# A dense layer's up products as 2x2 blocks with seven products for eight, on one core of Trainium2

## The chip, the core and the metric

The kernel runs on one core of a Trainium2 chip. A core has five engines with a row of instructions each: TensorE (PE: matmuls into PSUM; its weight loads are a row of their own, PEld), VectorE (DVE), ScalarE (ACT), GpSimd (POOL) and SyncE (SP), which issues the DMA transfers between the chip's memory and SBUF. Each engine takes its instructions in the order in which the program lists them and waits on semaphores for the others. The metric is the time of one execution on the device in microseconds, as the median of several executions.

## The reference, cut to what matters

Two layers, each a token mixer and a gated MLP with a convolution, on 1024 tokens of width 1024 with a hidden width of 22 x 128 = 2816, in float32. The change is in the second half of a layer and in the place of the modulations:

```python
for l in range(DEPTH):                                   # DEPTH = 2
    mod = (c_act @ w_mod[l] + b_mod[l])[:, None, :]
    sh1, sc1, g1, sh2, sc2, g2 = jnp.split(mod, 6, axis=-1)
...
    y = jnp.concatenate([oa, ob, oc, od], axis=-1) @ w_out[l]
    x = x + g1 * rms_norm(y, norm_g[l, 1])

    h = rms_norm(x, norm_g[l, 2]) * (1 + sc2) + sh2
    u = dwconv3(h @ w_up[l], ffn_conv[l])                # 1024 -> 2 x 2816, three taps along the tokens
    ug, uv = jnp.split(u, 2, axis=-1)
    y = (jax.nn.gelu(ug, approximate=True) * uv) @ w_down[l]
    x = x + g2 * rms_norm(y, norm_g[l, 3])
```

## The kernel before, in words

Features lie on the 128 partitions, tokens along the free dimension: a 128x1024 tile holds 128 features of all tokens, and "half 0" and "half 1" are the first and the last 512 tokens. Every float32 operand is held as two parts that TensorE can multiply, a high part and a low part. `split` (L108 to L111) makes them: ScalarE copies the high part (L110), and GpSimd or VectorE subtracts it for the low part (L111). A product is then three matmuls, high x high, high x low and low x high (`product`, L477, L478 and L481, and `mm3`, L468 to L470). The low and high parts of the normed input are the tiles `hh` and `hl`; the trace calls the tiles that share their room `hx` and `hp`.

The output projection of the mixer ends with the tiles `pw`. Then follow, for each half, a norm and a residual add (`residual`, L460 and L461), a second norm with modulation (`modulated`, L441 to L447) and the splits; a norm's sums over features are 8 or 7 matmuls with a tile of ones (L158), its scale a chain of small VectorE operations (`rstd`, L176 to L189). The modulated second half comes while TensorE does the first up products on half 0.

`ffn` goes over the 22 hidden tiles t in pairs. For a tile, a 1024x128 piece of the gate's weights and one of the value's are loaded (512 KB each) and split; 96 matmuls give both, 24 for each half of each; ScalarE copies PSUM to `u` (L1128); VectorE convolves both (`conv3`, L875 and L877), ScalarE applies the gelu (L1146), VectorE multiplies (L1147), and the result is split into `ah` and `al`. One pair later the down products of a pair run (`down_all`): eight output tiles of 128 features, 96 matmuls for each hidden pair, and VectorE adds each PSUM tile to the sums `y` (L1190). The last two pairs run by halves (`down`, L1168): half 0 of both, then the end of the layer for half 0, then half 1 of both, whose weights are still in SBUF, then its end. In layer 0 a half's end is a norm, the residual (written to memory, `xd`) and the modulated input of layer 1.

The modulations (`mod`, six pieces of 1024 per layer) are sums over eight rows of weights. `mod_sum` loads sixteen tiles of 256 KB (`mr`, two buffers, L357), eight for each of two sums, and VectorE adds them up (L360, L362); `mod_fold` transposes and reduces the two sums over the partitions (L402 to L416). In layer 0 six of them run in the background of the MLP: the last of layer 0 and five of layer 1.

The row of each engine is fixed when the program is built, by a scheduler that knows the program's order and the tiles' buffers; at run time it is not reordered. Pools give out their buffers in the order of the program, so an instruction can wait for a tile that is used by an unrelated earlier step.

## Time and profile before

| | |
|---|---|
| median of 3 executions | 3238.64 us (3237.59 to 3239.95) |
| the profiled execution's own time | 3236.76 us |
| its span, first to last instruction | 3234.9 us |
| granted TensorE clock, mean over the span | 0.974 |
| TensorE busy | 2985.9 us (92%) |
| VectorE, ScalarE, GpSimd busy | 63%, 33%, 30% |
| dense layer of layer 0, last `pw` to the last down product | about 869 to 1642 us |
| dense layer of layer 1 | about 2448 to 3216 us |

The profile shows one execution. Times of its rows count from the span's start. A busy share is an average over stages with different limits: TensorE's 92% holds stretches of 100% and stretches where it waits, and what a change in one stage is worth is read from that stage. Two instructions that follow each other on VectorE overlap by some 0.1 us, so a row with "x2" can be shorter than twice one.

### The profile page before, as it was taken

Reading aid. Unit: us, or ns where it says so; the run is one execution under the profiler, and the core shown is the slowest. Engines: PE = TensorE matmul, PEld = TensorE weight load, DVE = VectorE, ACT = ScalarE, POOL = GpSimd, SP = SyncE. Lnnn points to the kernel's source line nnn. Section 1 sums busy time; section 2 is a strip of 40 time slices with the busy share of each in tenths; the row PEclk is TensorE's granted clock in tenths of the full one; section 3 lists DMA queues with packets and bytes.
Section 4 is the critical chain, followed back from the end, with each engine's and each line's share of the span. In section 5 each row is a group of like instructions: output and inputs, shape, how many; then the busy total and the mean of one; then the engine's idle time right before and its main releaser. Section 6 shows DMA issues by size and latency. Waiting matters only on the chain. (4 is left out here: it accounts for less than half of the span.)

```text
span 3234.9 us, 35358 instructions
## 1 busy us (share of the span) xinstructions
PE 2985.9 (92%) x13706; PEld 2365.9 (73%) x13706; DVE 2029.7 (63%) x2849; ACT 1063.9 (33%) x1554; POOL 956.7 (30%) x712
## 2 busy tenths in 40 slices
PE   7888988988999999999988998898899999999997
PEld 3677767776677777788856886777676888888886
DVE  6687567698656666653587727568956434434347
ACT  4232443554332222212243324336534222222222
POOL 1221133324342322223232213142334422233222
PEclk9998999999999999999999998999999999999998
DMA  5235111103312433211131121110132111111113
GB/s 202 78 101 177 54 37 34 56 20 108 128 58 93 134 113 114 95 40 52 46 124 58 55 82 42 38 52 19 37 109 91 65 39 40 43 62 52 40 40 104
DMA packets 103091, 237.15 MB, mean 73 GB/s; under 512 B 11227, under 2 KB 29915, under 8 KB 102924
## 3 DMA queue, kind: packets, MB, share of 16 engines
q1 hardware_dynamic: 102924, 234.90, 22.4%
q8 instruction: 107, 1.75, 0.2%
q14 instruction: 60, 0.49, 0.1%
HBM read 205.59 MB, written 32.67 MB: 74 GB/s over the span
## 5 line engine op out<-in xcount | busy, mean ns | idle before, releaser
L111 POOL TENSOR_TENSOR wl<-raw,wh 128x1024 fp32r<-128x1024 f32 (+2 forms) x96 | 234.5, 2451 | 663.7 <-ACT wh L110 472.4
L477 PE MATMUL pj<-hp,uh 128*128 128x512 f32 x880 | 352.6, 401 | 1.6 <-ACT hp L442 1.6
L478 PE MATMUL pj<-hp,uh 128*128 128x512 f32 x880 | 347.1, 394 | 2.9 <-POOL hp L445 2.8
L477 PE MATMUL pj<-hh,wh 128*128 128x512 f32 x800 | 327.9, 410 | 14.2 <-DVE ql L526 8.5
L478 PE MATMUL pj<-hl,wh 128*128 128x512 f32 x800 | 323.2, 404 | 3.7 <-POOL hl L445 3.2
L481 PE MATMUL pj<-hp,ul 128*128 128x512 f32 x880 | 290.2, 394 | 0.0
L111 POOL TENSOR_TENSOR ul<-raw,uh 128x1024 fp32r<-128x1024 f32 x96 | 238.5, 2486 | 162.5 <-PE pj L481 84.7
L875 DVE TENSOR_SCALAR ta<-u,par 128x1024 f32<-128x1024 f32 (+1 forms) x46 | 55.9, 1216 | 356.1 <-ACT u L1128 324.0
L477 PE MATMUL pj<-hx,uh 128*128 128x512 f32 x528 | 212.5, 403 | 12.6 <-ACT u L1128 10.0
L110 ACT ACTIVATE wh<-raw 128x1024 fp32r<-128x1024 f32 (+2 forms) x104 | 107.2, 1047 | 345.1 <-PE po L469 242.8
L481 PE MATMUL pj<-hx,ul 128*128 128x512 f32 x528 | 209.8, 397 | 0.0
L478 PE MATMUL pj<-hx,uh 128*128 128x512 f32 x528 | 207.7, 393 | 0.0
L481 PE MATMUL pj<-hh,wl 128*128 128x512 f32 x800 | 206.5, 398 | 0.0
L477 PEld LDWEIGHTS pj<-hp,uh 128*128 128x128 f32 x880 | 165.6, 188 | 45.6 <-ACT hp L442 2.2
L478 PEld LDWEIGHTS pj<-hp,uh 128*128 128x128 f32 x880 | 165.5, 188 | 44.9 <-POOL hp L445 5.5
L481 PEld LDWEIGHTS pj<-hp,ul 128*128 128x128 f32 x880 | 165.2, 188 | 39.3 <-issue 1.0
L477 PEld LDWEIGHTS pj<-hh,wh 128*128 128x128 f32 x800 | 154.4, 193 | 54.0 <-issue 17.0
L110 ACT ACTIVATE uh<-raw 128x1024 fp32r<-128x1024 f32 x100 | 105.5, 1059 | 262.9 <-DMA raw<-in_w_up_dram 141.2
L1190 DVE TENSOR_TENSOR y<-y,po 128x1024 f32<-128x1024 f32 x96 | 117.0, 1219 | 110.6 <-PE po L470 110.6
L478 PEld LDWEIGHTS pj<-hl,wh 128*128 128x128 f32 x800 | 154.1, 193 | 41.8 <-POOL hl L445 5.4
L481 PEld LDWEIGHTS pj<-hh,wl 128*128 128x128 f32 x800 | 151.6, 190 | 34.6 <-issue 0.2
L1128 ACT ACTIVATE u<-pj 128x512 f32<-128x512 f32 x176 | 103.7, 593 | 209.1 <-PE pj L481 209.1
(375 smaller groups left out, 7120.2 us busy)
## 6 DMA issues: line engine op xcount, KB each, us to landing
raw<-in_w_up_dram SPq DMA_DIRECT2D x88, 512.0 KB, 3.5
mr<-in_w_mod_dram SPq DMA_DIRECT2D x144, 256.0 KB, 3.4
raw<-in_w_in_dram SPq DMA_DIRECT2D x52, 512.0 KB, 3.5
raw<-in_w_down_dram SPq DMA_DIRECT2D x44, 512.0 KB, 3.5
room<-in_w_mod_dram SPq DMA_DIRECT2D x48, 256.0 KB, 3.6
xd<-y SPq DMA_DIRECT2D x48, 256.0 KB, 2.4
raw<-in_w_out_dram SPq DMA_DIRECT2D x16, 512.0 KB, 3.9
x<-xd SPq DMA_DIRECT2D x14, 512.0 KB, 4.4
```

The lines of the kernel that those rows point to most:

```text
L110: self.nc.scalar.activation(hi, src, AF.Copy)
L111: (eng or self.nc.gpsimd).tensor_sub(lo, src, hi.bitcast(F32))
L477: nc.tensor.matmul(ps, wh[:, ks], self.hh[k][:, hs], start=k == 0, stop=False, skip_group_check=True)
L478: nc.tensor.matmul(ps, wh[:, ks], self.hl[k][:, hs], start=False, stop=False, skip_group_check=True)
L481: nc.tensor.matmul(ps, wl[:, ks], self.hh[k][:, hs], start=False, stop=k == KT - 1, skip_group_check=True)
L875: nc.vector.tensor_scalar(o, t[:, 0:n], cw(0), None, op0=ALU.mult)
L1128: nc.scalar.activation(u[:, 1 + 512 * half:513 + 512 * half], ps, AF.Copy)
L1190: self.mark = nc.vector.tensor_add(d, d, p)
```

## The change

The up products are regrouped. Let the 1024 input features be two halves (four tiles each) and the 1024 tokens two halves: the input is 2x2 blocks b11, b12, b21, b22, and the weights of a gate tile and a value tile are 2x2 blocks a11, a12, a21, a22. The product of two 2x2 block matrices is formed from seven block products, of sums of blocks, for eight. `dense_input` makes the normed second half into the sums t1 to t4 of input blocks (32 VectorE operations on 128x512, twelve GpSimd splits); `dense_up` goes over the 22 tiles: `sums` loads the gate's and the value's weights and makes the sums of weight blocks on VectorE (L1238 to L1243) with three or four splits; `begin` and `rest` issue seven quarters of twelve matmuls; five adds on VectorE combine them (L1268, L1275 to L1279). For the first five tiles `begin`, two of the quarters, is issued ahead. The gated tile is stored unsplit to memory (`actd`, L1289).

The down products form a second phase, `dense_down`, after all tiles: steps of two or four hidden tiles load weights and gated tiles, split them, multiply and add to `y`. In layer 0 the last eight hidden tiles are done by halves, four steps of two for half 0, then the end of the layer for half 0, then the same weights loaded once more for half 1. All background modulations move into this phase (six in layer 0, one in layer 1). A modulation's first sum stays on VectorE (L365, L367); its second is now scaled on ScalarE (L361) and added on GpSimd (L363); each of the two has one `mr` buffer of its own. The pool `fw` for weights has three buffers for four.

```diff
@@ mod_sum
-                    w = self.mr.tile([128, 512], F32, name="mr", tag="mr")
+                    w = self.mr.tile([128, 512], F32, name="mr", tag=f"mr{u}")
...
-                if k == 0:
+                if u and not room:
+                    nc.scalar.activation(w if k else acc, w, AF.Copy, scale=s)
+                    if k:
+                        nc.gpsimd.tensor_add(acc, acc, w)
+                elif k == 0:
@@ dense_input
+        n1, n2 = HALVES
+        self.t2, self.t3, self.t4w = [], [], []
+        for i in range(4):
+            j = 4 + i
+            a, b, t12 = y[i], y[j], temp("x")
+            t1, t2, t3, t4 = t12[:, n1], t12[:, n2], temp("sq"), temp("t")
+            normal(i)
+            normal(j)
+            shifted(j)
+            nc.vector.scalar_tensor_tensor(t1, a[:, n2], self.shift(l, 3, i), a[:, n1], op0=ALU.add, op1=ALU.subtract)
+            nc.vector.tensor_sub(t2, b[:, n2], t1)
+            nc.vector.tensor_sub(t4, b[:, n1], t2)
+            nc.vector.tensor_sub(t3, t2, a[:, n1])
+            self.split(self.hh[i][:, n2], self.hl[i][:, n2], t1, nc.vector)
+            self.split(self.hh[j][:, n2], self.hl[j][:, n2], b[:, n2])
+            for to, k, t, eng in ((self.t2, i, t2, None), (self.t4w, None, t4, nc.vector), (self.t3, j, t3, None)):
+                room = self.te.tile([128, 1024], F32R, name="t4", tag=f"t4{i}") if k is None else self.new_y(k, F32R)
+                self.split(room[:, n1], room[:, n2], t, eng)
+                to.append((room[:, n1], room[:, n2]))
@@ dense_up
+            def sums(t, whole):
...
+                nc.vector.tensor_add(s1, a21, a22)
+                nc.vector.tensor_sub(s2, s1, a11)
+                self.split(*w4, a22)
+
+                nc.vector.tensor_sub(a21, a11, a21)
+                nc.vector.tensor_sub(a22, a12, s2)
+                self.split(*w2, sums)
+                self.split(*w3, raw)
...
+                def tail(u):
+                    yb, z, w, u2 = (state[k] for k in ("y", "z", "w", "u2"))
+                    self.quarter(yb, w3, 0, t3, False)
+                    nc.vector.tensor_add(uv[:, c1], yb, u[:, c2])
+                    self.quarter(z, w3, 512, b22, False)
+                    nc.vector.tensor_add(u[:, c2], z, u2)
+                    nc.vector.tensor_add(uv[:, c2], uv[:, c2], uv[:, c1])
+                    nc.vector.tensor_add(uv[:, c1], uv[:, c1], w)
...
+            begun = [begin(early[t] if t < len(early) else self.up_weight(l, t)) for t in range(ahead)]
+            for t in range(FT):
+                w1, w2, w3, w4 = sums(t, t >= ahead)
+                if t < ahead:
+                    u, uv = begun[t], u_tile()
+                    head, tail = rest(u, w2, w3, w4, uv)
+                    head(u, t == 0)
+                else:
+                    uv = u_tile()
+                    head, tail = rest(None, w2, w3, w4, uv)
+                    u = begin(w1, head)
+                tail(u)
+                gated(t, (u, uv))
@@ dense_down
+            steps = [(2, "fwfw"), (4, "p" * 8), (4, "qqqqfwff")] + \
+                ([(2, "pppp")] * 4 if last else [(4, "p" * 8)])
+            mods = {0: (0, 5), 1: (1, 1), 2: (1, 0), 3: (1, 2), 4: (1, 4), 5: (1, 3)} if not last else {1: (1, 5)}
...
+            for n, names in steps:
+                ops = load(range(k, k + n), names)
+                whole(ops, k == 0)
+                part = background(step)
+                step += 1
+                if n == 4 and not last:
+                    part = background(step)
+                    step += 1
+                k += n
+            part = background(step)
...
+                final = [range(at, at + 2) for at in range(k, FT, 2)]
+                whole_half = slice(0, 512)
+                room = ("wwq", "qqq")
+                for j, ks in enumerate(final):
+                    some(load_half(ks, HALVES[0], room[j % 2]), HALVES[0], whole_half)
+                right.close()
+                end(HALVES[0])()
+                for j, ks in enumerate(final):
+                    some(load_half(ks, HALVES[1], room[j % 2]), HALVES[1], whole_half)
+                end(HALVES[1])()
```

In the program's order there are 528 matmuls fewer, all in the up products; the 1056 down products of each layer stay.

Three places in the rows of the engines. The first is TensorE at the head of layer 0's dense layer. `pj` and `po` are PSUM tiles of up products on half 0, `psc_6761` is the first block product on the sums t2 (which lie in the room of `y`). Before, the 96th product on half 0 is followed by the first one that needs half 1:

```order
L481 MATMUL pj_6615<-hp_5644,ul_6522 128x512
L481 MATMUL pj_6615<-hx_5637,ul_6522 128x512
L481 MATMUL pj_6615<-hp_5642,ul_6522 128x512
L477 MATMUL pj_6641<-hx_5634,uh_6342 128x512
L478 MATMUL pj_6641<-hx_5635,uh_6342 128x512
L477 MATMUL pj_6641<-hp_5636,uh_6342 128x512
```

After, 75 products on the way stand ahead of `psc_6761`, whose twelve need all four sums t2 (`y_6481` to `y_6550`), and the next products on half 0 (`pj_6638`, `hp_5638` and so on) come behind:

```order
L1184 MATMUL pj_6674<-hp_5636,wl_6666 128x512
L1263 MATMUL po_6762<-hx_5629,uh_6742 128x512
L1263 MATMUL po_6762<-hx_5630,uh_6742 128x512
L1263 MATMUL po_6762<-hx_5629,ul_6743 128x512
L1263 MATMUL psc_6761<-y_6481,uh_6742 128x512 x2
L1263 MATMUL psc_6761<-y_6481,ul_6743 128x512
L1263 MATMUL psc_6761<-y_6504,uh_6742 128x512 x2
L1263 MATMUL psc_6761<-y_6504,ul_6743 128x512
L1263 MATMUL psc_6761<-y_6527,uh_6742 128x512 x2
L1263 MATMUL psc_6761<-y_6527,ul_6743 128x512
L1263 MATMUL psc_6761<-y_6550,uh_6742 128x512 x2
L1263 MATMUL psc_6761<-y_6550,ul_6743 128x512
```

So the products that wait for the second half's norm moved ahead of 48 that do not (24 + 12 + 12 matmuls of `pj_6638`, `pj_6674` and `pj_6710`).

The second place is VectorE at the end of layer 0 for half 0. L176 takes the norm's sums out of PSUM, L178 is the first of its small operations. Before, they follow the last adds of half 0 (`pd`, L1168) directly:

```order
L1168 TENSOR_TENSOR y7_5674<-y7_5674,pd_11274 128x512
L171 TENSOR_TENSOR ta_11307<-ta_11307,tc_11324 128x512
L171 TENSOR_TENSOR ta_11307<-ta_11307,tb_11327 128x512
L176 STREAM_TRANSPOSE tn_11331<-po_11306 128x512
L1168 TENSOR_TENSOR y0_5667<-y0_5667,pd_11460 128x512
L178 TENSOR_SCALAR sm_11333<-tn_11331 128x16
```

After, L176 writes `tn_11368` 31 rows ahead of L178, and between them stand the end of one modulation and the whole of the last one, with its sum of eight tiles and its fold; the last rows of them:

```order
L367 SCALAR_TENSOR_TENSOR mc_10908<-mr_10927,cact_98,mc_10908 128x512
L367 SCALAR_TENSOR_TENSOR mc_10908<-mr_10930,cact_98,mc_10908 128x512
L407 STREAM_TRANSPOSE mr_10965<-mc_10908 128x512
L408 TENSOR_REDUCE sm_10966<-mr_10965 128x16
L407 STREAM_TRANSPOSE mr_10965<-mc_10933 128x512
L408 TENSOR_REDUCE sm_10966<-mr_10965 128x16
L410 COPY sm_10967<-sm_10966 64x32
L411 TENSOR_TENSOR sm_10966<-sm_10966,sm_10967 64x32
L412 COPY sm_10967<-sm_10966 32x32
L413 TENSOR_TENSOR sm_10966<-sm_10966,sm_10967 32x32
L415 COPY sm_10968<-sm_10966 32x8 x4
L178 TENSOR_SCALAR sm_11370<-tn_11368 128x16
```

So half 0's norm now stands behind all six modulations; `mc_10933`, the second sum, comes from the chain on ScalarE and GpSimd.

The third place is SyncE between the halves of layer 0. `xd` is the write of half 0's result, one for each of the eight `y`. Before, no weights of the dense layer are loaded here; the loads among these writes are layer 1's (`w_in`):

```order
L457 DMA raw_11365<-xd_82 128x2x512
L462 DMA xd_82<-y1_5668 128x512
L462 DMA xd_82<-y0_5667 128x512
L116 DMA raw_11759<-in_w_in_dram 128x1024
L462 DMA xd_82<-y2_5669 128x512
L462 DMA xd_82<-y3_5670 128x512
```

After, the first two down weights of half 1 stand there, the first behind two of the writes and the second behind all:

```order
L358 DMA mr_10961<-in_w_mod_dram 128x512
L506 DMA xd_82<-y_9608 128x512
L506 DMA xd_82<-y_9607 128x512
L116 DMA raw_11499<-in_w_down_dram 128x1024
L506 DMA xd_82<-y_9609 128x512
L506 DMA xd_82<-y_9610 128x512
L506 DMA xd_82<-y_9611 128x512
L506 DMA xd_82<-y_9612 128x512
L506 DMA xd_82<-y_9613 128x512
L506 DMA xd_82<-y_9614 128x512
L116 DMA raw_11505<-in_w_down_dram 128x1024
```

So the load without which half 1's first product can't be finished moved behind half 0's residual, and both behind the modulations' loads.

## Rows read from the trace of the kernel before

**Rows 1.** The page, part 1: busy time of each engine over the span.

```profile
PE 2985.9 (92%) x13706; PEld 2365.9 (73%) x13706; DVE 2029.7 (63%) x2849; ACT 1063.9 (33%) x1554; POOL 956.7 (30%) x712
```

**Rows 2.** Windows in the dense layers: length, busy time of each engine, clock, DMA.

```profile
core 0: us, PE busy (x) PEld busy (x) DVE busy (x) ACT busy (x) POOL busy (x), PEclk, DMA share, GB/s
2500.00:2900.00 400.00, 400.00 (x1715) 321.52 (x1714) 172.87 (x151) 92.95 (x111) 122.99 (x97) 1.00 0.15 48
900.00:1400.00 500.00, 487.75 (x2074) 389.41 (x2073) 330.16 (x386) 117.36 (x145) 152.87 (x118) 1.00 0.29 95
```

**Rows 3.** Timeline of VectorE in layer 1: start, duration, instruction, idle before.

```profile
2512.45 0.75 DVE L875 TENSOR_SCALAR ta<-u,par 128x1024 f32<-128x1024 f32 x1 [4.67 <-POOL al L111]
2513.24 2.61 DVE L877 SCALAR_TENSOR_TENSOR ta<-u,par,ta 128x1024 f32<-128x1024 f32 x2
...
2542.13 0.68 DVE L1188 COPY y<-psc 128x512 f32<-128x512 f32 x1
...
2574.66 2.34 DVE L875 TENSOR_SCALAR ta<-u,par 128x1024 f32<-128x1024 f32 x1 [16.28 <-ACT u L1128]
```

**Rows 4.** Timeline of GpSimd at the same places.

```profile
2514.69 3.42 POOL L111 TENSOR_TENSOR ul<-raw,uh 128x1024 fp32r<-128x1024 f32 x1 [2.28 <-ACT uh L110]
...
2542.25 2.39 POOL L111 TENSOR_TENSOR al<-ta,ah 128x1024 fp32r<-128x1024 f32 x1 [3.16 <-ACT ah L110]
...
2574.06 2.40 POOL L111 TENSOR_TENSOR ul<-raw,uh 128x1024 fp32r<-128x1024 f32 x1 [4.81 <-PE pj L481]
```

**Rows 5.** Windows at the head of layer 0's dense layer.

```profile
868.00:902.00 34.00, 31.57 (x107) 19.27 (x106) 17.53 (x38) 12.73 (x22) 11.12 (x12) 1.00 0.26 93
902.00:936.00 34.00, 31.74 (x132) 24.27 (x131) 22.05 (x22) 16.69 (x23) 15.72 (x12) 1.00 0.10 31
```

**Rows 6.** Timelines of VectorE and GpSimd there, first and last rows of the modulated half.

```profile
901.95 2.08 DVE L441 SCALAR_TENSOR_TENSOR t<-y,gm,acc 128x512 f32<-128x512 f32 x3
...
911.77 0.75 DVE L447 SCALAR_TENSOR_TENSOR hx<-t,mod,hx 128x512 fp32r<-128x512 f32 x1
...
905.48 3.05 POOL L445 TENSOR_TENSOR hp<-t,hp 128x512 fp32r<-128x512 f32 x2 [10.10 <-ACT t L444]
912.24 2.72 POOL L445 TENSOR_TENSOR hp<-t,hp 128x512 fp32r<-128x512 f32 x2 [3.71 <-ACT t L444]
```

**Rows 7.** Groups by line and shape, 900 to 1640 us: DVE, POOL, ACT.

```profile
L877 DVE SCALAR_TENSOR_TENSOR ta<-u,par,ta 128x1024 f32<-128x1024 f32 x42 | 53.9, 1284 | 1.3
...
L111 POOL TENSOR_TENSOR al<-ta,ah 128x512 fp32r<-128x512 f32 x2 | 2.6, 1296 | 3.4 <-ACT ah L110 3.4
...
L1128 ACT ACTIVATE u<-pj 128x512 f32<-128x512 f32 x86 | 50.3, 592 | 86.0 <-PE pj L481 86.0
```

**Rows 8.** DMA issues, 900 to 1640 us: count, size, median us to landing.

```profile
raw<-in_w_down_dram SPq DMA_DIRECT2D x20, 512.0 KB, 3.6
```

**Rows 9.** Timeline of VectorE in a modulation sum of before.

```profile
1014.30 1.53 DVE L362 SCALAR_TENSOR_TENSOR mc<-mr,cact,mc 128x512 f32<-128x512 f32 x2
1017.92 0.75 DVE L362 SCALAR_TENSOR_TENSOR mc<-mr,cact,mc 128x512 f32<-128x512 f32 x1 [2.09 <-DMA mr<-in_w_mod_dram]
```

**Rows 10.** Timeline of GpSimd, half 0's residual adds at layer 0's end.

```profile
1626.39 1.68 POOL L461 TENSOR_TENSOR y<-y,raw 128x512 f32<-128x512 f32 x1 [20.54 <-DVE y L460]
...
1638.19 1.30 POOL L461 TENSOR_TENSOR y<-y,x 128x512 f32<-128x512 f32 x1 [4.19 <-DMA x<-xd]
```

**Rows 11.** Timeline of VectorE in a fold, first and last row.

```profile
979.04 0.70 DVE L402 STREAM_TRANSPOSE mr<-mc 128x512 f32<-128x512 f32 x1
...
984.30 0.17 DVE L416 TENSOR_TENSOR mod<-sm,par 128x8 f32<-128x8 f32 x1
```

**Rows 12.** Timeline of TensorE where half 1's down products follow half 0's.

```profile
1635.87 0.50 PE L468 MATMUL pd<-ah,wh 128*128 128x512 f32 x1 [1.24 <-DVE y L1168]
```

**Rows 13.** Timeline of VectorE, first operation of half 0's norm at layer 0's end.

```profile
1621.61 0.16 DVE L178 TENSOR_SCALAR sm<-tn 128x16 f32<-128x16 f32 x1
```

**Rows 14.** Window at the start of layer 1.

```profile
1640.00:1700.00 60.00, 44.78 (x136) 25.64 (x135) 52.91 (x81) 30.28 (x46) 24.90 (x17) 0.91 0.32 114
```

297 lines of the change are left out of this document (182 added, 115 removed).

## The prediction

> **What bounds the kernel now.** I read the page first: TensorE is busy for 2985.9 of 3234.9 us and no other engine for more than 63% [rows 1]. The windows say more. In the dense layer of layer 1 all 400 us of a stretch are busy, 1715 products in it, and VectorE needs 43% of them [rows 2]: a 128x512 product costs 400 / 1715 = 0.233 us, and only fewer products or a hole in their row can change the time there. In layer 0 the same code runs 2074 products in 500 us where 2144 would fit; VectorE is 66% busy there, since it does the modulation sums beside the convolution. So 70 x 0.233 = 16 us are already lost in layer 0 to a VectorE that comes late, at 66% busy and with GpSimd at 31%.
>
> Why late at 66%: VectorE and GpSimd stand in each other's way. A 128x1024 split on GpSimd takes 2.40 us alone and 3.42 us where two of VectorE's multiply-adds run when it starts; it ends 2.3 us after the second of them [rows 3, 4]. The other way round, a multiply that costs VectorE 0.75 us takes 2.34 us when it comes 0.6 us after a split began, and ends 0.54 us behind it. A copy out of PSUM beside a split keeps its 0.68 us [rows 3, 4]. So an operation of VectorE on SBUF alone and a split exclude each other here, and their times add.
>
> **The change, part by part, against 3236.8 us of the profiled execution.** The numbers of products come from the order of instructions.
>
> *Fewer products.* 84 for 96 per hidden tile, 22 tiles, two layers: 528 less, 264 a layer. 264 x 0.233 = 61.5 us a layer is the ceiling, 123 in all. The 1056 down products of a layer stay.
>
> *The head of the dense layer.* Before, from 868 to 936 us TensorE issues 107 + 132 = 239 matmuls, 14 of them sums for the norm, so 225 products [rows 5]: 96 of them need only the first half of the tokens and fill the time in which the second half is normed. After, 75 stand ahead of the first block sums (order, first piece); 48 more that would be ready stand behind. The block sums need the sum t2 of all four pairs of tiles with its split. The second norm ends at 901.95 us; then the old VectorE work takes until 912.5, GpSimd's until 915.0 [rows 6]: 12 operations of 0.67 us and four of 1.3 us, and 13 us is just their plain sum. The new work is 32 such operations on VectorE and 12 splits on GpSimd. Up to the last t2 that is 30 x 0.67 + 11 x 1.3 = 34 us if they exclude each other, 20 if not. By [rows 3, 4, 6] I take 32; with three weight sums that VectorE does first (2 us) the block products start near 902 + 2 + 32 = 936. TensorE has then done 75 products where before it had 225: 150 x 0.233 = +35 us a layer (bounds +23 and +37).
>
> The Trainium skill, "SBUF — State Buffer", section "Who interferes with whom", says that a VectorE instruction with two SBUF inputs, or in a two-port mode, and a GpSimd instruction that reads SBUF lock each other out for the whole instruction, and that one SBUF input does not. The trace agrees (3.42 against 2.40 us, and 0.68 out of PSUM); by the rule the head would be the full +37, and rival 2 below would be out.
>
> *Up products, first five tiles.* Their first quarters are ready, so a tile is 60 products, 14.0 us. VectorE needs per tile: four weight sums and one add at 0.67, two multiplies at 0.75, four multiply-adds and a product at 1.28 [rows 3, 6, 7], 11 us on SBUF alone, and four adds out of PSUM at 0.68, 2.7 us. GpSimd has two splits of 2.4 and one of 1.3, 6.1 us. 11 + 6.1 = 17 us exceed the 14.0. The 48 late products cover a part: I take +8 us a layer (0 to 20).
>
> *The other 17 tiles.* 84 products, 19.6 us. GpSimd has one split more: 11 + 8.5 = 19.5 us of work that excludes itself, and 22 if VectorE's PSUM adds never fall beside a split. At 19.6 TensorE would just stay the bound. Before, with 66% and 31%, TensorE lost 2.4% [rows 2]; now it is 70% and 43%. 3% of 333 us: +10 us a layer (5 to 42). Layer 0 gets its 16 us back, since the modulations leave this stretch.
>
> *Second phase.* Gated tiles go to memory and come back, 512 KB each. The first step's 96 products (22 us) cover eight loads of the second step at about 3.6 us from issue to landing [rows 8], which overlap, and their splits: +5 us a layer (2 to 10). The later steps have 192 x 0.233 = 45 us each for the same loads, so they cost nothing.
>
> *The modulations in layer 0.* This is the largest term. All six now run beside 1056 down products. One of their two chains goes through one buffer: load, scale on ScalarE, add on GpSimd, next load. Before, VectorE starts a pair of multiply-adds at 1014.30 that takes 1.53 us, so the first buffer is free near 1015.07, and its next load has landed at 1017.92 [rows 9]: 2.85 us. With 0.59 on ScalarE, 1.28 on GpSimd [rows 7] and 0.2 for two handoffs a step takes 4.9 us; bounds are 4.5, without the handoffs and a load sooner, and 5.8, with the 1.68 of a contended add [rows 10] and half a microsecond more of load. Seven steps, a first scaling of 0.6, and 2.5 us until the fold has freed the sums (the whole fold takes 5.4 us, [rows 11]) make 38 us a modulation. The first fold waits for the second step's last add, 5 + 288 x 0.233 = 72 us after the up products; the sixth modulation folds at 72 + 5 x 38 + 5 = 267 us. TensorE by itself would have finished half 0 at 5 + 864 x 0.233 = 206. VectorE's row holds the last modulation ahead of half 0's norm (order, second piece): half 0's end waits for it. +60 us (30 to 105).
>
> *Between the halves.* Before, the weights of the last pairs lie in SBUF and TensorE pauses for 1.24 us [rows 12]. After, half 1's weights are loaded anew, and the second one stands behind all writes of half 0's result on SyncE (order, third piece). From the norm's first operation at 1621.61 to the last residual add, 1639.49, before took 18 us [rows 10, 13]; then a load of 3.6 [rows 8], ScalarE about 1.1 (twice the 0.59 of half the width), GpSimd 2.4. Without half 1's adds in between I take 23 us (15 to 27).
>
> *Next layer's start.* Half 0's tiles are ready long before half 1 ends. Before, TensorE got 136 matmuls through in 60 us at a clock of 0.91 there [rows 14] where 257 fit; about half of the lost 28 us returns: -14 (0 to -25).
>
> **Sum.** Layer 1: -61.5 + 35 + 8 + 10 + 5 = -3.5. Layer 0: the same, -16, +60, +23, -14, so +49.5. Together +46: 3283 for the profiled execution; the median lies 1.9 us above the profiled time: **3285 us**.
>
> **Rivals.**
> 1. *The modulations hide (faster).* If a modulation takes less than (206 - 72 - 5) / 5 = 26 us, 3.3 us a step, half 0 ends at TensorE's pace and the 60 us go: 3225. For it: ScalarE and GpSimd overlap the other chain, and a load alone may land sooner. Against it: a single buffer with 2.85 us of load in each turn.
> 2. *VectorE and GpSimd mostly miss each other (faster).* Head +23 for 35, the tiles +5 in all for 18: 25 less a layer: 3235, and 3225 if the second phase's loads cost nothing too. With rival 1: 3170. Against it: three pairs of rows that all show the exclusion, and a head of before that is the plain sum.
> 3. *They meet all the time.* 22 us a late tile instead of 20, and the first ones at their bound: +32 + 12 a layer: 3373, and 3330 at half of it. For it: 70% and 43% make more than 100% together, which before had nowhere for long. Against it: a fifth of VectorE's work comes out of PSUM.
> 4. *A step of the chain takes 5.8 us* (contended adds): 45 us a modulation, +35: 3320.
>
> **How the numbers follow.** Forecast (3245 to 3325) 0.43; rival 1 0.15; rival 2 0.16; both 0.08; rival 3 0.11; rival 4 0.07. A measurement tells about 0.2%, 6.5 us, from no change. Below 3232 lie two thirds of rivals 1 and 2, both together, and the edge of the forecast: 0.30. Within 0.2% lies what is left of rivals 1 and 2, 0.09; above, 0.61. The range leaves out the case of both faster rivals and the upper half of rival 3: 3185 to 3340; the forecast's own is 3245 to 3325.
>
> **What will show it.** After each layer's output projection a hole of 25 to 35 us in TensorE's row, ending with a sum out of SBUF named y or x. In windows of the up products VectorE near 70% and GpSimd above 40%, TensorE 95 to 98%. Between the last half-0 add of layer 0 and the norm's first operation some tens of us in which VectorE waits for loads of modulation weights, at 5 us a turn. Then some 20 us without products before half 1. Layer 1's dense layer about as long as before. I am wrong if layer 0's half 0 ends within 210 us of the last up product, if the head's hole is under 20 us, or if the period of a late tile is far from 20 us.

## The result, and the profile after

The changed kernel takes 3336.72 us (median of 4 runs, 3333.9 to 3339.0) against 3238.11 us for the kernel before on the same chip: 1.0303 times, with an interval of 1.0285 to 1.0321. Slower was forecast, and the time lies inside the range, but the loss is 98.6 us where the forecast had 46.

The page of the changed kernel, part 1, answers to [rows 1]:

```profile
PE 2895.6 (87%) x13178; PEld 2296.9 (69%) x13178; DVE 2380.3 (71%) x3203; ACT 1167.9 (35%) x1698; POOL 1244.5 (37%) x853
```

TensorE has the 528 matmuls less that were counted (13706 in [rows 1]) and is busy 90 us less, while the span is 98.6 us longer (3333.5 for 3234.9 us). So some 190 us more of the span are holes. Windows along layer 0 show where they are (columns as in [rows 2]; the first line is the end of the output projection, the next two the head of the dense layer, then the first tiles and a late one; the last lies between the halves):

```profile
860.00:880.00 20.00, 13.08 (x43) 9.14 (x42) 7.87 (x10) 13.27 (x24) 8.49 (x6) 0.83 0.14 47
920.00:940.00 20.00, 5.25 (x8) 2.29 (x9) 20.00 (x19) 9.74 (x16) 13.21 (x9) 0.50 0.00 0
940.00:960.00 20.00, 15.19 (x50) 11.17 (x50) 7.62 (x10) 6.85 (x11) 9.68 (x14) 0.69 0.17 53
980.00:1000.00 20.00, 15.51 (x61) 12.26 (x61) 17.85 (x20) 5.18 (x7) 6.06 (x11) 0.91 0.23 80
1020.00:1040.00 20.00, 17.70 (x64) 13.96 (x63) 18.47 (x17) 5.71 (x7) 12.05 (x9) 0.84 0.19 65
1040.00:1060.00 20.00, 20.00 (x86) 16.29 (x85) 18.94 (x16) 4.58 (x7) 11.85 (x9) 0.97 0.27 93
1640.00:1660.00 20.00, 0.00 (x0) 0.00 (x0) 3.94 (x5) 2.88 (x4) 5.96 (x4) 0.50 0.31 103
```

At 0.233 us a product 20 us hold 86. The head has 8 and 50, a first tile's stretch 61 to 64, a late tile's 86 although VectorE is busy for 18.9 of 20 us there. Between the halves there is a window without a single product. VectorE, GpSimd and ScalarE are idle for most of it as well, and the granted clock stands at 0.50, that is 1.2 GHz; TensorE had run nothing since 1620.

TensorE's timeline at three places: ahead of the dense layer, from the up to the down products, and between the halves (in brackets: idle before, and for whom):

```profile
869.00 0.80 PE L512 MATMUL pw<-hx,oh 128*128 128x512 f32 x1 [6.92 <-ACT y L1145]
...
876.56 0.40 PE L514 MATMUL pw<-hp,ol 128*128 128x512 f32 x1
...
1384.81 0.50 PE L512 MATMUL po<-wh,uh 128*128 128x512 f32 x1 [2.40 <-DVE y L1359]
...
1690.36 0.80 PE L512 MATMUL pd<-qh,wh 128*128 128x512 f32 x1 [69.92 <-ACT wh L110]
```

The down products follow the up products at once; the pause in their first step is small (2.40 us, for VectorE's addition to y). The one between the halves is 69.92 us, by far the longest; next come 10.93 us at 1506.91, for an addition to y that stands in VectorE's row behind a modulation's fold, and 9.53 us at 1618.38, for the sums of half 0's norm. The first, 6.92 us in the output projection ahead of the dense layer, no step of the prediction had. In the kernel before the projection's last product starts at 865.92:

```profile
865.92 0.40 PE L470 MATMUL pw<-hp,ol 128*128 128x512 f32 x1
```

Measured from the first to the last product of a place (starts, in the two traces), the loss splits so:

| stretch | before | after | difference | forecast |
|---|---|---|---|---|
| start of layer 0's output projection | 743.84 | 747.37 | +3.5 | 0 |
| the two output projections | 122.1, 122.0 | 129.2, 128.9 | +13.9 | 0 |
| layer 0, dense layer (last projection product to last down product) | 775.3 | 880.4 | +105.1 | +63.5 |
| from there to layer 1's output projection | 682.7 | 673.0 | -9.7 | -14 |
| layer 1, dense layer | 769.5 | 755.1 | -14.5 | -3.5 |

Inside layer 0's dense layer the up products take 497.3 us from the last projection product; the terms of the prediction give 501 there (70 us from 865.92 to the block products at 936, 1773 more products of 0.233 us, and its 8 and 10 us). So the excess lies behind them. VectorE's timeline of the folds (the second transpose of each of the first two and the last two modulations) and of the norm of half 0:

```profile
1447.67 0.71 DVE L407 STREAM_TRANSPOSE mr<-mc 128x512 f32<-128x512 f32 x1
1498.12 0.71 DVE L407 STREAM_TRANSPOSE mr<-mc 128x512 f32<-128x512 f32 x1 [8.01 <-POOL mc L363]
...
1633.07 0.71 DVE L407 STREAM_TRANSPOSE mr<-mc 128x512 f32<-128x512 f32 x1 [4.68 <-POOL mc L363]
1674.95 0.71 DVE L407 STREAM_TRANSPOSE mr<-mc 128x512 f32<-128x512 f32 x1 [4.59 <-POOL mc L363]
1677.98 0.17 DVE L178 TENSOR_SCALAR sm<-tn 128x16 f32<-128x16 f32 x1
```

The last up product starts at 1373.63, so the first fold is at 74 us (72 forecast), as the prediction had it, and the norm at 304 where it had 267. The error up to the norm is in the five periods between folds: 1674.95 - 1447.67 = 227 us, 45.5 us each for 38. GpSimd's timeline shows what a period holds, in the second modulation and in the last:

```profile
1459.94 1.30 POOL L363 TENSOR_TENSOR mc<-mc,mr 128x512 f32<-128x512 f32 x1 [2.20 <-ACT mr L361]
1462.47 2.40 POOL L111 TENSOR_TENSOR pl<-pl,ph 128x1024 fp32r<-128x1024 f32 x1 [1.23 <-ACT ph L110]
1464.84 2.86 POOL L111 TENSOR_TENSOR pl<-raw,ph 128x1024 fp32r<-128x1024 f32 x1
1467.65 2.42 POOL L111 TENSOR_TENSOR wl<-raw,wh 128x1024 fp32r<-128x1024 f32 x1
1470.02 1.75 POOL L363 TENSOR_TENSOR mc<-mc,mr 128x512 f32<-128x512 f32 x1
...
1652.08 1.70 POOL L363 TENSOR_TENSOR mc<-mc,mr 128x512 f32<-128x512 f32 x1 [3.69 <-ACT mr L361]
1657.44 1.74 POOL L363 TENSOR_TENSOR mc<-mc,mr 128x512 f32<-128x512 f32 x1 [3.67 <-ACT mr L361]
```

Where nothing else runs, a step takes 4.9 us (an add of 1.26) to 5.4 us (an add of 1.7 beside VectorE's multiply-add): within the bounds of 4.5 to 5.8. The scalings of the last modulation stand at 1635.84 and 1672.86, seven steps of 5.3 us. But beside the products the engines' rows also hold the splits of the tiles that the second phase loads. Here three of them on GpSimd, 7.7 us, stand between two adds that are 10.1 us apart: the load between them is issued at 1461.27, ScalarE copies a weight tile at 1465.00 before it scales the load at 1465.96, and GpSimd splits for another 3.3 us before it adds.

The splits are the smaller part of the error, though. SyncE, ScalarE and VectorE at the start of the second modulation:

```profile
1455.51 0.80 SPq L358 DMA_DIRECT2D mr<-in_w_mod_dram  x2
```

```profile
1448.42 0.72 ACT L361 ACTIVATE mc<-mr,cact 128x512 f32<-128x512 f32 x1
...
1459.14 0.73 ACT L361 ACTIVATE mr<-mr,cact 128x512 f32<-128x512 f32 x1 [3.89 <-DMA mr<-in_w_mod_dram]
```

```profile
1455.00 0.48 DVE L365 TENSOR_SCALAR mc<-mr,cact 128x512 f32<-128x512 f32 x1
```

The chain's first scaling leaves its buffer free at 1449.14, but the next load into it is issued at 1455.94, as the second of SyncE's two: in SyncE's row it stands 0.43 us behind the next load for VectorE's chain, and that one waits until VectorE, behind the last fold, has read the single buffer of that chain (L365). The two chains, meant to run side by side, are tied at this place in all five modulations: the load comes 6.8, 4.6, 1.7, 2.6 and 1.8 us after its buffer was free.

From the first to the second scaling the five modulations take 10.7, 8.4, 5.5, 7.5 and 5.6 us, 37.6 in all where five steps of 4.9 are 24.5: 13 us. The other thirty steps take 166 us for 147, 19 more: 6 for the two steps with the rows of splits shown, 6 for 13 of the 35 adds that take 1.7 to 1.8 us for 1.3, the rest mostly for loads that land later beside the second phase's. Fold and first scaling take the last 5 of the 37 us. The prediction summed the chain that has its engines, and SyncE, for itself.

### The profile page after: what moved, and what is told of

The parts are those of the page before. It is cut to its first block, busy times and chain, and to the rows that moved or that the text cites. A ratio compares the mean times of both kernels' runs of the same rounds, so it can differ in the third digit from the quotient of the medians.

```text
span 3333.5 us, 35440 instructions
## 1 busy us (share of the span) xinstructions
PE 2895.6 (87%) x13178; PEld 2296.9 (69%) x13178; DVE 2380.3 (71%) x3203; ACT 1167.9 (35%) x1698; POOL 1244.5 (37%) x853
## 5 line engine op out<-in xcount | busy, mean ns | idle before, releaser
L111 POOL TENSOR_TENSOR wl<-raw,wh 128x1024 fp32r<-128x1024 f32 (+1 forms) x87 | 217.3, 2499 | 462.9 <-ACT wh L110 271.3
L681 PE MATMUL po<-s,v 128*96 128x128 f32 (+3 forms) x672 | 130.4, 355 | 42.0 <-ACT s L678 41.8
L681 PE MATMUL po<-hp,v 128*96 128x256 f32 x512 | 128.2, 407 | 29.4 <-ACT hp L678 29.0
L110 ACT ACTIVATE wh<-raw 128x1024 fp32r<-128x1024 f32 (+1 forms) x95 | 99.0, 1044 | 146.9 <-PE pj L522 75.6
L681 PEld LDWEIGHTS po<-s,v 128*96 128x96 f32 x672 | 97.9, 185 | 69.7 <-ACT s L678 54.6
L568 ACT ACTIVATE qh<-pj 64x512 fp32r<-64x512 f32 x128 | 107.1, 837 | 98.8 <-PE pj L525 53.3
L111 POOL TENSOR_TENSOR ul<-raw,uh 128x1024 fp32r<-128x1024 f32 x43 | 112.7, 2621 | 49.5 <-ACT uh L110 49.3
L921 DVE SCALAR_TENSOR_TENSOR tb<-u,par,tb 128x1024 f32<-128x1024 f32 x88 | 127.0, 1443 | 0.0
L363 POOL TENSOR_TENSOR mc<-mc,mr 128x512 f32<-128x512 f32 x49 | 69.7, 1422 | 152.9 <-ACT mr L361 152.9
L367 DVE SCALAR_TENSOR_TENSOR mc<-mr,cact,mc 128x512 f32<-128x512 f32 x49 | 52.9, 1079 | 100.9 <-DMA mr<-in_w_mod_dram 100.8
L668 PE MATMUL psc<-qh,ks 128*128 128x256 f32 (+2 forms) x272 | 88.5, 339 | 36.4 <-DVE s L796 15.3
L921 DVE SCALAR_TENSOR_TENSOR ta<-u,par,ta 128x1024 f32<-128x1024 f32 x88 | 114.2, 1297 | 0.0
```

Source lines behind the costliest of these rows:

```text
L110: self.nc.scalar.activation(hi, src, AF.Copy)
L111: (eng or self.nc.gpsimd).tensor_sub(lo, src, hi.bitcast(F32))
L363: nc.gpsimd.tensor_add(acc, acc, w)
L568: nc.scalar.activation(self.perm(qh[h][o:o + 64], r)[:, n * half:n * half + n, :], src, AF.Copy)
L668: nc.tensor.matmul(ps, ks[:, c], qh[:, q0:q1], start=first, stop=False, skip_group_check=True)
L681: nc.tensor.matmul(o[0:96, co], v(tt, h), s[:, cs], start=co.start // 512 not in seen, stop=False, skip_group_check=True)
```

## The experiments

Ratios are to the kernel before, which ran beside each of them (medians of 3240.6 to 3243.1 us); 0.001 is 3.2 us, and "less" is the difference to the changed kernel's 1.0303; with both intervals such a difference is good to 6 to 10 us.

### The modulations, all but taken out

```diff
-            for k in range(KT):
+            for k in range(KT if room else 1):
```

Left out: seven of the eight weight tiles of each background modulation, so that the sums hold one tile's part.

> This run leaves out seven of the eight weight tiles of each sum of the background modulations; nothing else changes. In the changed kernel half 0's norm of layer 0 starts 304 us after the last up product and TensorE stands still for 70 us before half 1. Theory A (the chain of the modulations holds half 0's end): half 0's norm starts 210 to 235 us after the last up product, the hole of 70 us shrinks to some 20 to 25 us (the load of half 1's weights), and the time falls by 65 to 95 us, to 3240 to 3270. Rival B (the hole comes from half 1's weights loaded anew and from the loads of the second phase, not from the modulations): the hole stays over 45 us and the time falls by less than 30 us, to 3305 or more.

Measured: 3240.93 us, 1.0000 (0.9988 to 1.0013), 98 us less (96 by the medians), a little more than theory A gave. TensorE's timeline between the halves:

```profile
1596.22 0.80 PE L512 MATMUL pd<-qh,wh 128*128 128x512 f32 x1 [13.30 <-ACT wh L110]
```

The hole of 69.92 us shrinks to 13.30, below the 20 to 25 expected, and the norm of half 0 comes 213 us after the last up product, where the products alone would give 206. The modulations cost 98 us, not 60; without them the change costs nothing and gains nothing.

### A second buffer for GpSimd's chain alone

```diff
-                    w = self.mr.tile([128, 512], F32, name="mr", tag=f"mr{u}")
+                    w = self.mr.tile([128, 512], F32, name="mr", tag=f"mr{u}", bufs=1 + u)
```

> The second chain of a modulation (load, scale on ScalarE, add on GpSimd) gets two buffers instead of one; the first chain keeps one. Theory A (each step of the second chain pays a whole load, 2.85 of 4.9 to 5.4 us): the second chain's steps fall to 2 to 3 us, the first chain with its 3.6 us a step becomes the longer, a modulation takes 33 to 36 us instead of 45 on average, half 0's norm starts 245 to 265 us after the last up product instead of 304, and the time falls by 40 to 60 us, to 3275 to 3297. Rival C (SyncE's row, which issues both chains' loads in turn, or the DMA itself sets the step): steps stay at 4.5 us and more, the time moves by less than 15 us.

Measured: 1.0265 (1.0241 to 1.0289), 12 us less; neither theory's number. The periods of the folds are 48.9, 46.6, 41.0, 42.5 and 34.1 us, so only the last came where the buffer theory put them. VectorE's chain still goes through one buffer: in the third modulation its multiply-adds stand 3.6 to 7.0 us apart and mostly wait for their loads. SyncE still ties the chains too: in the third modulation both of GpSimd's buffers are free by 1497.4, and their next loads are issued at 1505.37 and 1505.84, behind the one for VectorE's chain at 1504.95. The norm of half 0 starts 293 us after the last up product, not 245 to 265. That both chains have to be relieved is what this suggests; the next two kernels do that.

### Both sums on one side, with shared buffers

The first kernel gives both chains to ScalarE and GpSimd with three shared buffers, the second gives both to VectorE with two, as the kernel before has them:

```diff
-                    w = self.mr.tile([128, 512], F32, name="mr", tag=f"mr{u}")
+                    w = self.mr.tile([128, 512], F32, name="mr", tag="mr0", bufs=3)
...
-                if u and not room:
+                if not room:
...
```

> Both sums of each background modulation go to ScalarE (scale) and GpSimd (add), through three shared buffers in place of two chains with one buffer each. Theory A, the turn of a single buffer (load, scale or multiply-add, next load) paces the modulations in both chains: with three buffers a step costs what GpSimd's add costs, 1.3 to 1.8 us, so a modulation takes 16 x 1.3 to 1.8 plus 5 for fold and handoff, 26 to 34 us in place of 45; the end of layer 0's half 0 comes 60 to 80 us sooner against the last up product and the whole kernel gains 50 to 80. Rival B, the in-order rows of the engines (VectorE's additions of the down products, the splits of the loaded tiles) set the period: GpSimd now has 16 adds more in its row and a modulation stays above 40 us, gain under 20. Rival C, the loads themselves (256 KB each, 96 of them) are as fast as they get beside the down products' loads: period above 40 us too, but with ScalarE waiting for loads and not GpSimd for ScalarE.

> Undoes one part of the change: both sums of a background modulation on VectorE alone through two shared buffers, as the kernel before has them; ScalarE and GpSimd have no part. Theory A (buffer turns): 16 steps, each half of a turn of 2.85 us load plus 0.75 us, so 1.8 to 2.2 us a step, 34 to 40 us a modulation with the fold, 20 to 50 us sooner than the changed kernel. Rival B (in-order rows): VectorE's row has the additions of the down products between and does eight more multiply-adds, so a modulation stays at 45 us or above and the kernel is the same or up to 30 us slower.

Measured: 1.0173 (1.0159 to 1.0188) on GpSimd, 42 us less; 1.0209 (1.0194 to 1.0224) on VectorE, 30 us less. The mean period of the folds is 33.7 us in the one and 38.5 in the other, both inside what the buffer theory gave (26 to 34, 34 to 40). The gain of the first stays under its 50 to 80 although its period is right: of the 59 us that the five periods save, 12 are lost before the first fold (86 us after the last up product for 74) and 12 behind the last (the norm comes 15 us after it for 3). VectorE's timeline there, and TensorE's:

```profile
1583.33 0.71 DVE L407 STREAM_TRANSPOSE mr<-mc 128x512 f32<-128x512 f32 x1 [15.54 <-POOL mc L363]
```

```profile
1584.76 0.77 PE L512 MATMUL pd<-qh 128*128 128x512 f32 x1 [11.30 <-DVE y L1366]
```

The fold stands in VectorE's row and waits 15.54 us for GpSimd; the additions to y stand behind it, and TensorE waits 11.30 us for one of them. So single buffers, with the loads that waited for them in SyncE's row, paced the modulations, and when they no longer do, the engines' rows come next.

### Weights that stay for both halves

```diff
-                for j, ks in enumerate(final):
-                    some(load_half(ks, HALVES[0], room[j % 2]), HALVES[0], whole_half)
+                ops = load(range(k, FT), "wwqqqqff")
                 right.close()
+                some(ops, HALVES[0], HALVES[0])
                 end(HALVES[0])()
-                for j, ks in enumerate(final):
-                    some(load_half(ks, HALVES[1], room[j % 2]), HALVES[1], whole_half)
+                some(ops, HALVES[1], HALVES[1])
                 end(HALVES[1])()
```

The modulations are shortened as in the first experiment, and the last four gated tiles go through the halves in place of the last eight, so four more go through whole steps.

> To be compared with mod_short, in which seven of eight weight tiles of the background modulations are left out (here too). Beside that, the last eight gated tiles and their weights of layer 0 stay in SBUF for both halves of the tokens, as in layer 1, so nothing is loaded between the halves. If the second load prices the stretch between the halves as the prediction says (23 us without products; 13.3 us measured in mod_short, and stalls behind it): 12 to 22 us less than mod_short. Rival: the next layer starts when half 0 is normed, and what half 1 loses comes back there: within 5 us of mod_short.

Measured: 0.9941 (0.9928 to 0.9955), 19 us less than the first experiment, inside the 12 to 22. The rival is half right all the same: layer 0's dense layer gets 41 us shorter (788.0 to 747.2 us, by the measure of the table above), and 21 of them come back ahead of layer 1's output projection (673.7 to 694.3). Since fewer tiles go by halves, too, the 19 us are the price of the second load and of this together; no run parts them.

### Order at the head, and the engine of its splits

The first kernel puts the 48 products on half 0 ahead of the block sums, as ready ones; the second moves twelve of the block sums' splits in each layer from GpSimd to VectorE.

```diff
-                    head(u, t == 0)
+                    with (tc.issue_after(begunmm.ins) if t == 0 else ExitStack()):
+                        head(u, t == 0)
...
```

> The 48 products that need only half 0 are put ahead of the first block sums at the head of both dense layers; the same instructions, another order on TensorE. Theory A (TensorE stands still in front of the block sums while products are ready behind them): 48 products of 0.233 us move into the hole, 11 us a layer: the time falls by 18 to 24 us, to 3313 to 3319. Rival D (the tiles after the head are bound by VectorE and GpSimd anyway, so that what is won is lost again by the fifth tile): less than 8 us in all.

```diff
-            self.split(self.hh[j][:, n2], self.hl[j][:, n2], b[:, n2])
+            self.split(self.hh[j][:, n2], self.hl[j][:, n2], b[:, n2], nc.vector)
-            for to, k, t, eng in ((self.t2, i, t2, None), (self.t4w, None, t4, nc.vector), (self.t3, j, t3, None)):
+            for to, k, t, eng in ((self.t2, i, t2, nc.vector), (self.t4w, None, t4, nc.vector), (self.t3, j, t3, nc.vector)):
```

> The twelve splits of block sums at the head, which GpSimd does, go to VectorE: 44 operations there, none on GpSimd. In the changed kernel the head's work from the first operation after the second norm to the last split of t2 takes 31.6 us. Theory A (VectorE and GpSimd exclude each other, so their times add anyway): about 42 operations of 0.62 to 0.67 us up to the last t2, 26 to 28 us, 4 us less a layer; the time falls by 4 to 10 us. Rival E (they mostly run beside each other and something else made the head long): the time to the last t2 rises to 35 us or more and the kernel gets slower by 6 to 15 us.

Measured: 1.0332 (1.0308 to 1.0357), no gain, for the order, if anything 9 us slower; 1.0276 (1.0254 to 1.0298), 9 us less, for the splits on VectorE. The first doesn't test what it was meant to test. TensorE's timeline of that kernel at the head, and ScalarE's of the changed kernel:

```profile
944.84 0.79 PE L1180 MATMUL pj<-hp,uh 128*128 128x512 f32 x1 [32.39 <-ACT u L1219]
```

```profile
945.11 0.58 ACT L1218 ACTIVATE u<-pj 128x512 f32<-128x512 f32 x1
```

The hole is still there, 32.39 us in one piece (32.37 in layer 1), and the first of the 48 ends it: they were not ready. They need the PSUM tile `pj`, whose copy to SBUF stands in ScalarE's row behind the block sums' copies; in the changed kernel it comes at 945.11, as late as the block sums, although the products in `pj` were done by 914. So the sentence ahead of the prediction that these 48 don't wait for the second half's norm doesn't hold, and whether products in the hole would pay stays open: no run moved that copy.

The second agrees with exclusion. From the norm to the last t2 the head takes 26.9 us with every split on VectorE, within the 26 to 28 of theory A, where two engines need 31.6, and the up products are 7.4 and 3.9 us shorter in the two layers. In the changed kernel VectorE's timeline at the head reads

```profile
921.52 1.75 DVE L111 TENSOR_TENSOR t<-t,t 128x512 fp32r<-128x512 f32 x1
923.19 1.75 DVE L482 SCALAR_TENSOR_TENSOR x<-y,mod 128x512 f32<-128x512 f32 x1
924.87 1.75 DVE L462 SCALAR_TENSOR_TENSOR y<-y,gm,acc 128x512 f32<-128x512 f32 x1
926.54 0.68 DVE L483 TENSOR_TENSOR x<-y,x 128x512 f32<-128x512 f32 x1
```

and GpSimd's at the same time

```profile
921.01 1.71 POOL L111 TENSOR_TENSOR y<-x,y 128x512 fp32r<-128x512 f32 x1
922.68 1.71 POOL L111 TENSOR_TENSOR y<-sq,y 128x512 fp32r<-128x512 f32 x1
924.36 1.71 POOL L111 TENSOR_TENSOR hp<-y,hp 128x512 fp32r<-128x512 f32 x1
```

An operation of 0.68 us takes 1.75 while GpSimd splits, one of GpSimd's 1.26 takes 1.71, and they alternate: one of each every 1.68 us. At 926.54, with GpSimd idle, it is 0.68 again. The Trainium skill's rule that was cited in the prediction ("SBUF — State Buffer", "Who interferes with whom") says this of two SBUF inputs, and these rows agree but for a rest: the pair takes 1.68 us where the two alone take 0.68 and 1.26, together 1.94, so some 0.26 us overlap.

### Shifts on VectorE

```diff
-                shifted(k)
+                if k % 2:
+                    shifted(k)
+                else:
+                    nc.vector.tensor_scalar(y[k][:, hs], y[k][:, hs], self.shift(l, 3, k), None, op0=ALU.add)
```

> In the norm of half 0 ahead of the dense layer, the shift of every second tile goes from ScalarE to VectorE (four of eight a layer). Theory E: the output projection ends 8.6 us late in each layer because the copy of its sums out of PSUM stands behind sixteen shifts and splits on ScalarE; with four fewer of 0.6 us the copy comes 2 to 4 us sooner and TensorE's hole of 6.9 us there shrinks as much, and less of the low clock behind it: 2 to 8 us a layer, 4 to 16 in all. Rival F: VectorE's multiplications by norm and gain (1.0 to 1.3 us each beside GpSimd) set the pace of that chain and ScalarE waits for them: the shifts on VectorE delay the chain, no gain, within 4 us or slower.

Measured: 1.0272 (1.0254 to 1.0290), 10 us less, inside the 4 to 16. TensorE's last projection product:

```profile
865.58 0.40 PE L517 MATMUL pw<-hp,ol 128*128 128x512 f32 x1
```

ScalarE's copy that frees PSUM for the projection's last products, in the changed kernel and in this one:

```profile
868.37 0.57 ACT L1145 ACTIVATE y<-pw 128x512 f32<-128x512 f32 x1
```

```profile
859.40 0.58 ACT L1148 ACTIVATE y<-pw 128x512 f32<-128x512 f32 x1
```

The projections last 120.2 and 119.4 us, 9 less each than in the changed kernel, so their lateness came from ScalarE's row: the copy out of PSUM stood behind all sixteen of half 0's shifts and splits, and now stands behind two of the splits. The scheduler moved it, so it gained 9 us where four shifts less had been put at 2 to 4. Of the 18 us only 10 show in the time: the up products start sooner but take 500.5 us, for TensorE now waits 3.54 us for ScalarE's squares (L164) in the second half's norms.

### Smaller steps with more buffers, and the edits together

In layer 0 the second phase goes in nine steps of two gated tiles; the pool of eight pairs shrinks to four, and the room gives each chain four buffers and two modulations' sums. The resident tiles are in as well.

```diff
-            steps = [(2, "fwfw"), (4, "p" * 8), (4, "qqqqfwff")] + \
-                ([(2, "pppp")] * 4 if last else [(4, "p" * 8)])
...
+                steps = "fwfw pppp qqqq fwfw pppp qqqq pppp fwfw pppp".split()
+                starts = {0: ((0, 5), (1, 1)), 1: ((1, 0),), 3: ((1, 2),), 4: ((1, 4),), 6: ((1, 3),)}
+                folds = 1, 3, 4, 6, 7, 8
...
```

> In layer 0 the second phase goes in nine steps of two gated tiles, so four pairs of tiles are enough where eight were; the room gives each of the two modulation chains four weight buffers and two modulations' sums in flight, the folds are spread over the steps up to the last, and the last four gated tiles with their weights stay in SBUF for both halves. Theory A (single buffers pace the modulations, the second load prices the stretch between the halves): the modulations hide behind the products as in mod_short, -96 us, and the resident tiles give the -19 of short_res: 110 to 120 us less than the changed kernel, some 20 below the kernel before (3215 to 3232 us). Rival B (the engines' rows, VectorE above all, which now adds nine times in place of five, cannot take the modulations in 206 us): half 0 ends 230 us or more after the last up product, and the kernel is 3250 us or above.

The same with the splits of the head and the shifts on VectorE:

> fine, with the two edits that gained by themselves: the twelve splits of the head on VectorE (-9) and every second shift of half 0's norm on VectorE (-10). If the three causes lie in different places, they add: 15 to 22 us less than fine. Rival: both edits relieve the same wait (the head of the dense layer is late by the projection or by the block sums, whichever comes last), and together they give no more than one: 8 to 11 us less than fine.

And with the first tap of the gated convolution on ScalarE:

```diff
-        nc.vector.tensor_scalar(o, t[:, 0:n], cw(0), None, op0=ALU.mult)
+        nc.scalar.activation(o, t[:, 0:n], AF.Copy, scale=cw(0))
```

> best, with the first tap of the gated convolution (two multiplications a tile, 1.3 us and less on VectorE) on ScalarE. Theory D (the first five tiles of a layer are bound by VectorE and GpSimd, which exclude each other, 61 to 65 products in 20 us at VectorE 18 to 19 of 20): each of them gets 1.5 us shorter, 5 to 10 us a layer, 10 to 20 in all, less than best. Rival G (they wait for the chain of one tile, weights' sums to splits to products to convolution, and not for VectorE's load): within 5 us of best, or slower, since ScalarE's first tap hands over to VectorE.

Measured: 1.0064 (1.0050 to 1.0077), 77 us less, where 110 to 120 were expected; 0.9995 (0.9983 to 1.0007) with the two edits, 22 less again, so these add, and the 9 and 10 us, each at the edge of the noise, are clear of it together; 0.9997 (0.9986 to 1.0007) with the tap, no gain. The last one leaves open what paces the first five tiles: it isn't the load of VectorE alone. In the first one theory A failed and rival B's two numbers came true: half 0's norm comes 271 us after the last up product, and the time is 3262.64 us. TensorE's timeline in the second phase of the kernel with the two edits shows why:

```profile
1393.37 0.76 PE L515 MATMUL po<-ph 128*128 128x512 f32 x1 [6.25 <-DVE y L1362]
...
1441.78 0.79 PE L515 MATMUL psc<-qh 128*128 128x512 f32 x1 [4.24 <-DVE y L1362]
```

PSUM stays full until VectorE gets to its addition to y. VectorE's row was full; the last pair of kernels asks of what.

### Less on VectorE, or less on GpSimd

The first kernel takes six steps of three tiles (three rounds of additions less on VectorE, GpSimd's work unchanged, one modulation for each step, three buffers a chain); the second also moves the second chain to VectorE, both chains alternating over the six buffers (more for VectorE, less for GpSimd).

```diff
-                steps = "fwfw pppp qqqq fwfw pppp qqqq pppp fwfw pppp".split()
+                steps = ["fwfwqq", "pppppp"] * 3
...
```

```diff
-                    w = self.mr.tile([128, 512], F32, name="mr", tag=f"mr{u}")
+                    w = self.mr.tile([128, 512], F32, name="mr", tag=f"mr{k % 2}")
...
-                if u and not room:
+                if False:
```

> best, with layer 0's second phase in six steps of three gated tiles in place of nine of two (six additions of the down products to y in place of nine: 30 x 1.2 us and 12 x 0.7 us less on VectorE), one modulation for each step, three buffers a chain. In best, TensorE waits 5 times 4 to 6 us for VectorE's additions to y in that phase, VectorE busy 18 to 20 of 20 us there. Theory H (VectorE's own row is full there: additions, folds, chain): the phase loses 20 to 35 us less, 20 to 35 us below best. Rival I (what fills the row is the wait of multiply-adds for GpSimd's splits and adds, which stay the same): 0 to 12 below best. Rival J (a weight's load is late and blocks the additions queued behind it): no change, or slower, since a modulation now has 34 us and starts at a step's begin.

> trio, with both sums of a modulation on VectorE (8 more multiply-adds of 0.75 us each, 6 us a modulation) through six shared buffers and none on ScalarE and GpSimd (8 adds of 1.28 us less, 10 us a modulation, which exclude VectorE's SBUF work). Rival I (exclusion fills the row): 6 x 4 us of the exclusive sum go, 10 to 25 below trio. Theory H (VectorE's own busy time): 36 us more on VectorE, the same as trio or up to 30 slower.

Measured: 0.9980 (0.9970 to 0.9989), 5 us less than the nine-step kernel with the two edits, at the edge of what the intervals part, and 0.9935 (0.9921 to 0.9948), 15 less again. Both numbers are rival I's; for the first, no change (rival J) isn't excluded. Windows of 200 us in the second phase, in the nine-step kernel with the two edits, then the two:

```profile
1380.00:1580.00 200.00, 170.60 (x683) 135.73 (x682) 165.10 (x179) 58.68 (x70) 112.99 (x62) 0.91 0.56 185
```

```profile
1380.00:1580.00 200.00, 181.27 (x759) 146.33 (x758) 157.26 (x168) 67.26 (x80) 121.57 (x64) 0.95 0.60 200
```

```profile
1380.00:1580.00 200.00, 190.02 (x799) 153.17 (x798) 175.90 (x226) 39.39 (x38) 67.88 (x28) 0.97 0.64 214
```

The third has the busiest VectorE of the three, with 226 instructions for 168, and the most products, 799. GpSimd's busy time fell from 121.57 to 67.88 us, and VectorE's rows got shorter with it. Its multiply-adds of the modulations in the same windows of the two kernels (count, busy time, mean ns):

```profile
L367 DVE SCALAR_TENSOR_TENSOR mc<-mr,cact,mc 128x512 f32<-128x512 f32 x36 | 36.1, 1002 | 5.7 <-DMA mr<-in_w_mod_dram 5.5
```

```profile
L367 DVE SCALAR_TENSOR_TENSOR mc<-mr,cact,mc 128x512 f32<-128x512 f32 x79 | 63.5, 818 | 2.4 <-DMA mr<-in_w_mod_dram 2.0
```

One takes 0.75 us alone, so VectorE's busy time holds waits for GpSimd, and a load that TensorE can stand isn't read from it alone. The sum of the two engines (278, 279, 244 of 200 us) falls with the second edit; with the first it stays although the products go from 683 to 759, so it isn't a measure by itself either. The second edit also frees ScalarE of the chain's scalings and ends the tie between the two chains' loads, so its 15 us are not shown to be GpSimd's alone. This kernel, 3222.19 us against 3242.3, is faster than the kernel before.

## Why the prediction came out as it did

Direction and range were right; the step that failed is the modulations in layer 0, "38 us a modulation ... +60 us". Half 0's norm came 304 us after the last up product, not 267, and removing the modulations gave 98 us, so that term was mis-sized by 37 or 38 us. Its parts:

- The mechanism, one buffer whose turn holds load, scaling and add, was right, and the plain step too (4.9 to 5.4 us for 4.9, with the contended add that was kept for rival 4).
- What was left out is the rest of the rows that the chain goes through. The largest part is SyncE's: the two chains were summed as if they ran side by side, but a load of the one stands behind a load of the other, which waits for VectorE and its fold. The first step of a modulation took up to 10.7 us, which makes 13 of the 37 us. This is read from the trace; no run unties the loads and leaves the rest. The splits of the loaded tiles, which the prediction had hidden from TensorE, are not hidden from the chain, but cost it some 6 us.
- The last period, with no split left, is 41.9 us, still 4 above the 38: contended adds in four of its seven steps, and its first load 1.8 us late.
- The first fold (74 for 72 us) was right, so the error is five periods of 7.5 us.

Step by step for the rest:

- *Fewer products*: 528 less, as counted.
- *Head and tiles*: 501 us by the terms, 497.3 measured, but the parts are wrong, so that the sum fits is luck. The block sums take 31.6 us (914.77 to 946.35) for the 32 forecast. They begin at 915, not 904, because the projection ends 10.6 us later. The price was put as 75 products in the row where 225 had been, with 48 more ready; those 48 were not ready. The late tiles, costed at +10, cost nothing: 86 products in 20 us with VectorE at 18.9. The first five cost more than their 8, some 16: 61 to 65 in 20 us.
- *Output projection*: not in the prediction at all, 7 us a layer. In half 0's norm ScalarE has sixteen operations where it had twelve (L442 and L444 before), and the copy that TensorE waits for stands behind all of them; before it stood behind five.
- *Between the halves*: from the norm's first operation half 1 was to take 23 us of loads and 192 x 0.233 = 45 us of products, 68. It takes 79 (1677.98 to 1756.98): the first product comes 12 us after the norm, not 23, but the products then take 67 us, with 15 us of waits between them (6.08 and 3.98 the longest, for splits of the loads) and a granted clock of 0.88 on average.
- *Next layer's start*: -14 forecast, -9.7.
- *Layer 1*: -3.5 forecast, -14.5. Its up products take 494.6 us where the terms give the same 501; the rest lies behind them.

Rival 1, modulations that hide, didn't happen; a step of 3.3 us would have been needed. With smaller steps and four buffers they would have hidden by the sum of the first experiment and of the resident tiles (117 us less), and came to 77: 40 us are left, of which moving GpSimd's chain to VectorE takes 15. Rival 2 falls with the head, which took 31.6 us, not 20, though the late tiles went as it had them. Rival 3's late tile of 22 us didn't come. Rival 4 had 45 us a modulation (its own step of 5.8 gives 43.7), and 45.5 were measured, but not for its reason: 22 of the 35 adds were not contended.

What stays open is the first five tiles: a VectorE lighter by the first tap doesn't shorten them, and whether earlier products would was not tested. TensorE waits there for VectorE's add of the block sums (L1268), 3.14 us at 983.30.

## What to carry to other kernels

When work is moved onto a chain through one buffer, sum the whole row of each engine in its turn, with what stands there for other reasons, and SyncE's row first: a load that stands behind another chain's load waits for that chain's engine too. A split that TensorE never waits for still holds the buffer. Where VectorE and GpSimd both work on SBUF, a busy share of either holds waits for the other: here it paid to move work from GpSimd, busy for 61% of the stretch, to VectorE, busy for 79%. An operation that is added to an engine's row also delays the copies out of PSUM that stand behind it, and TensorE with them: at the end of the projection, and at the head, where products that looked ready were not.

## What was not expected of the hardware

VectorE's rows lengthen while it waits for GpSimd, so its busy share is no load: 18.9 of 20 us at a late tile cost TensorE nothing, and 157 of 200 us with GpSimd at 122 go with 759 products where 200 / 0.233 = 858 fit. After the hole between the halves products of half 1 start 0.43 us apart from 1696.14 on, at a granted clock of 0.52 between 1695 and 1700 (1.2 GHz is 0.50), where they start 0.23 us apart at full clock; 15 of the 192 do, so this costs some 3 us behind the hole.
